# A Hymba decoder layer on one core: the output projection with w_out split once and its tiles one by one

## The chip, the cores and the metric

The kernel runs on one core of a Trainium2 chip. The metric is the device time of one execution in microseconds, the median of several runs. The engines are named as the profile names them: PE (matmuls; PEld is its weight load), DVE and POOL (element-wise on vectors), ACT (scalar functions and copies) and SP, which here issues the DMAs.

## The reference

One decoder layer, x of 1024 rows (S) by 1024 columns (D), all in float32:

```python
proj = x @ w_in                                   # 3072 columns: q, k, v, gate B, gate C, h
attn = rmsnorm(softmax(q1 k1^T) v - lam * softmax(q2 k2^T) v)   # 4 heads, causal
conv = B * causal_dwconv3(C * h)
mix  = concat([attn, conv], -1) @ w_out           # 512 + 512 columns, w_out is 1024 x 1024
h1   = layer_norm(ALPHA * x + mix, ln1_g, ln1_b)
up   = h1 @ w_up                                  # 2 x 2816 columns: gate, value
f    = (silu(causal_dwconv3(gate) + cb) * value) @ w_down
out  = layer_norm(ALPHA * h1 + f, ln2_g, ln2_b)
```

## The kernel before, in words

**Products.** Every float32 operand is split into a "hi" part, rounded to the type that PE takes (a cast on ACT, L63), and a "lo" part, the rest (a subtraction on DVE, or on POOL where `eng` says so, L64). A product is three matmuls, hi by hi, hi by lo and lo by hi (`mm3`, L72 to L74). The large products go by 2x2 blocks in seven products instead of eight (`pair`, L103 ff.). For the FFN the seven operands of h1 are "11", "21", "22" and the differences "t1", "t2", "t3", "t4", each a hi and a lo tile of `[128, 4, 512]` in `hb`. In them h1 stands transposed (its columns on the partitions).

**Order.** The code is written in one order and a scheduler places each engine's instructions; each engine then runs its own list in order. Tiles live in pools, and an instruction that writes a tile waits until the tile that held the memory before has been read.

**The output projection** (from L517 on) takes cat, the concatenation, from eight DRAM blocks `cat_d[k]` of 128 columns each, stored by the attention (`cat_d[0..3]`, L371) and by the convolution (`cat_d[4..7]`, `gate_out`, L471 and L472). `cat_d[3]` and `cat_d[7]` are the last to be stored. The k-blocks are taken in `K_ORDER = (4, 5, 0, 1, 2, 6, 7, 3)`. Row tiles of 128 rows stand in three groups, of tiles 0 to 2, 3 to 5 and 6 to 7. Each group goes over all eight k: `weights` (L591) loads w_out's block k (L593) and splits it in two halves, the group's part of cat is loaded (L612) and split into `ch` and `cl`, and each tile gets six matmuls into its two PSUM banks. `REUSE = 2` blocks are kept from one group to the next, so 20 of the 24 times a block is loaded and split again; in the third group five of them split their lo on POOL (`POOL_LO`). The second group goes over k in the reverse order. After a group, each tile's sum (L635: ALPHA x + the product), its layer norm (L539 to L547) and its turning follow, put off into the next group at three places (`NORM_AT`).

**The turning.** `first_half` (tiles 0 to 3) transposes a tile's eight 128x128 blocks on PE (L552) and splits them into "11" and "21". `second_half` and `combine` (tiles 4 to 7) transpose too and make the differences from the transposed blocks: old values are put together again on POOL (L573), t1, t2 and t3 are DVE subtractions out of PSUM, t4 is on POOL. For tiles 5 to 7 that waits until after the early gates.

**The early gates.** The FFN's first four pairs (`NEARLY = 4`) need only "11" and "21" for their gate half; those 96 matmuls run before the operands of the second half are done. Pair 0's sums `s1_0` and its difference are prepared there (`wu0` is its w_up block). Then pairs 0 to 21 run whole, and the down projection follows.

**The start.** x's eight tiles `xt`, in the right-hand pool `ini`, feed the operands `xb` of the input projection. Then the pairs of the input projection run interleaved with the attention, with their temporaries (s1, p1, ...) in the pool `wab`.

Of the kernel before, what the change touches and what calls it, by code (L numbers as in the profile page):

```python
# [46 lines left out]
def layer_kernel(ctx: ExitStack, tc: tile.TileContext, x, xt, w_in, w_v, lam, vecs, w_out, ln, w_up, w_down, out):  # L47
# [507 lines left out]
    def first_half(src, t):  # L555
        ts = slice(t * P, (t + 1) * P)
        for k0, n in ((0, "11"), (4, "21")):
            split(hb[n][0][:, :, ts], hb[n][1][:, :, ts], transposed(src, k0))

    def second_half(src, t):  # L560

        b_ = [transposed(src, k0) for k0 in (0, 4)]
        return lambda: combine(t, *b_)

    def combine(t, b12, b22):
        ts = slice((t - 4) * P, (t - 3) * P)

        def put(n, v, eng=None):
            split(hb[n][0][:, :, ts], hb[n][1][:, :, ts], v, eng=eng)

        def old(n, tag, bufs=1):
            v = cp.tile([P, 4, P], F32, name=f"o{n}", tag=tag, bufs=bufs)
            G.tensor_tensor(v, hb[n][0][:, :, ts].bitcast(F32), hb[n][1][:, :, ts].bitcast(F32), op=ALU.add)  # L573
            return v

        t1 = old("11", "tb0", 2)
        t4 = old("21", "tb2")
        V.tensor_tensor(t1, b12, t1, op=ALU.subtract)
        put("t1", t1)
        t2 = cp.tile([P, 4, P], F32, name="t2", tag="tb1")  # L580
        V.tensor_tensor(t2, b22, t1, op=ALU.subtract)
        put("t2", t2)
        put("22", b22)
        t3 = cp.tile([P, 4, P], F32, name="t3", tag="tb0", bufs=2)
        A.copy(t3, b12)
        V.tensor_tensor(t3, b22, t3, op=ALU.subtract)
        put("t3", t3)
        G.tensor_tensor(t4, t4, t2, op=ALU.subtract)
        put("t4", t4, G)

    def weights(t0, k, eng):  # L591
        raw = e0.tile([P, D], F32, name=f"wo{t0}_{k}_r", tag="wg", bufs=NWG)
        SQ.dma_start(raw, w_out[k * P:(k + 1) * P, :])  # L593
        wo = [e0.tile([P, 2, 512], F32R, name=f"wo{t0}_{k}_{d}", tag="ring", bufs=RING[0]) for d in range(2)]
        for d in range(2):
            split(wo[d][:, 0, :], wo[d][:, 1, :], raw[:, d * 512:(d + 1) * 512], eng=eng)
        return wo

    pending, late, held = [], [], {}
    for t0 in (0, 3, 6):  # L600
        tt = list(range(t0, min(t0 + 3, NT)))
        w = len(tt) * P
        acc = {(t, d): bank(f"op{t}_{d}") for t in tt for d in range(2)}
        order = K_ORDER if t0 != 3 else K_ORDER[::-1]
        for ki, k in enumerate(order):
            if ki < REUSE and t0:
                wo = held[k]
            else:
                wo = weights(t0, k, G if ki in POOL_LO and t0 == 6 else None)
            held[k] = wo  # L610
            cr = cc.tile([P, 384], F32, name="cr", tag="cr", bufs=4)
            SQ.dma_start(cr[:, :w], cat_d[k][:, t0 * P:t0 * P + w])  # L612
            ch = cc.tile([P, 384], F32R, name="ch", tag="ch", bufs=2)
            cl = cc.tile([P, 384], F32R, name="cl", tag="cl", bufs=2)
            split(ch[:, :w], cl[:, :w], cr[:, :w])
            if ki == 0:
                xr = {}
                for t in tt:
                    xr[t] = cx.tile([P, D], F32, name=f"xr{t}", tag="xr", bufs=4)
                    SQ.dma_start(xr[t], x[t * P:(t + 1) * P, :])  # L620
            if ki == 1 and t0 == 0:
                g1 = bcast_row(cp, 0, "g1")
                b1 = bcast_row(cp, 1, "b1")
            for i, t in enumerate(tt):
                s_ = slice(i * P, (i + 1) * P)
                for d in range(2):
                    mm3(acc[t, d], ch[:, s_], cl[:, s_], wo[d][:, 0, :], wo[d][:, 1, :], ki == 0, ki == 7)
            if pending and ki in NORM_AT:
                pending.pop(0)()
        while pending:  # L630
            pending.pop(0)()
# [327 lines left out]
```

## Time and profile before

| | us |
|---|---|
| median of 3 runs (1128.56 to 1128.86) | 1128.77 |
| the profiled execution | 1129.07 |
| span of its core in the trace | 1127.3 |
| PE busy | 1084.9 |
| DVE busy | 906.4 |
| ACT busy | 522.5 |
| POOL busy | 147.6 |

The span is what the trace covers; the profiled execution's own time is 1.8 us longer. Matmuls overlap in PE's pipeline: one that is listed with 0.39 us starts 0.23 us after the one before it, and a busy PE is not PE at its peak. In a row of the waits, the engine and the line that waited stand ahead of the arrow and the one waited for behind it. The granted clock of 1.00 is 2.4 GHz, 0.50 is 1.2 GHz.

### The profile page before, as it was taken

To read this page: it belongs to the slowest core of one execution; us is meant where nothing else is said; L and a number is where in the kernel's file an instruction comes from. 1 tells how busy PE (TensorE), PEld (TensorE's weight loads), DVE (VectorE), ACT (ScalarE), POOL (GpSimd) and SP (SyncE) were. 2 spreads that over 40 slices of the span, in tenths; PEclk is the share of its full clock that TensorE was granted. 3 is DMA by queue.
4 is the path that set the end of the run, shared out by engine and by line. 5 is a ranking of instruction groups with operands and counts; after the bars stand their busy time and mean duration, and the time that the engine had idled before them with its cause. 6 is when DMAs were issued, how large, how long until landed. Compare 5 with 4: busy or idle time off the path is not lost.

```text
span 1127.3 us, 13854 instructions
## 1 busy us (share of the span) xinstructions
PE 1084.9 (96%) x4940; PEld 873.8 (78%) x4940; DVE 906.4 (80%) x1393; ACT 522.5 (46%) x980; POOL 147.6 (13%) x182
## 2 busy tenths in 40 slices
PE   7999999999999999879999999999999999999996
PEld 6777877876768888668888888888888887788885
DVE  7678898689787688998967676777777599997797
ACT  6357586386675333445433334333333333444540
POOL 0002213013031224760000000000000000000102
PEclk9999999999999999999999999999999999999998
DMA  7421201301206754423232212131312295111111
GB/s 267 150 94 43 85 25 52 115 21 52 75 29 197 279 177 159 154 75 113 94 112 70 99 59 109 57 113 57 112 56 93 78 383 220 38 66 38 46 67 75
DMA packets 50421, 118.53 MB, mean 105 GB/s; under 512 B 5040, under 2 KB 18480, under 8 KB 50352
## 3 DMA queue, kind: packets, MB, share of 16 engines
q1 hardware_dynamic: 50352, 117.64, 29.7%
q8 instruction: 39, 0.64, 0.2%
q14 instruction: 30, 0.25, 0.1%
HBM read 90.88 MB, written 26.74 MB: 104 GB/s over the span
## 4 chain that ended last, share of the span: by engine, by line
PE 71%; DVE 15%; ACT 5%; POOL 3%; DMA 3%; issue 2%; SPq 0%; POOLq 0%; DVEq 0%; ACTq 0%
PE X L74 8%; PE X L72 8%; PE X L73 8%; PE Z L74 5%; PE Z L73 5%; PE Z L72 5%; PE dx L73 2%; PE dx L74 2%; PE dx L72 2%; PE op L74 2%; PE op L73 2%; PE op L72 2%; DVE a L64 2%; PE dz L74 2%; PE dz L72 2%
## 5 line engine op out<-in xcount | busy, mean ns | idle before, releaser
L64 DVE TENSOR_TENSOR a<-s,a 128x512 fp32r<-128x512 f32 x118 | 85.3, 724 | 45.3 <-ACT a L63 44.3
L63 ACT CAST a<-s 128x512 fp32r<-128x512 f32 x118 | 73.3, 623 | 94.5 <-PE X L74 43.0
L63 ACT CAST a<-w 128x512 fp32r<-128x512 f32 x106 | 65.9, 623 | 87.3 <-PE X L74 40.4
L64 DVE TENSOR_TENSOR a<-w,a 128x512 fp32r<-128x512 f32 x102 | 72.3, 710 | 22.6 <-ACT a L63 22.2
L63 ACT CAST T<-b 128x512 fp32r<-128x512 f32 x66 | 40.6, 621 | 68.4 <-PE dz L74 33.9
L73 PE MATMUL dx<-T,S 128*128 128x512 f32 x176 | 69.0, 392 | 1.2 <-DVE T L64 1.2
L74 PE MATMUL dx<-T,S 128*128 128x512 f32 x176 | 68.5, 389 | 0.0
L72 PE MATMUL dx<-T,S 128*128 128x512 f32 x176 | 66.0, 391 | 0.0
L64 DVE TENSOR_TENSOR T<-b,T 128x512 fp32r<-128x512 f32 x66 | 45.0, 685 | 16.3 <-ACT T L63 16.3
L74 PE MATMUL op<-wo,cl 128*128 128x512 f32 x128 | 51.2, 400 | 3.2 <-DVE cl L64 3.2
L444 DVE TENSOR_REDUCE nm<-sc 128x1 f32<-128x128 f32 (+5 forms) x64 | 47.5, 750 | 7.7 <-PE sc L443 7.3
L709 POOL MEMSET gs<- 128x2 f32 x22 | 2.2, 99 | 379.6 <-DVE t L728 379.6
L73 PE MATMUL dz<-T,S 128*128 128x512 f32 x132 | 51.8, 393 | 0.0
L74 PE MATMUL dz<-T,S 128*128 128x512 f32 x132 | 51.5, 390 | 0.0
L72 PE MATMUL op<-wo,ch 128*128 128x512 f32 x128 | 51.3, 401 | 0.0
L448 ACT ACTIVATE p<-sc,nm 128x128 f32<-128x128 f32 (+5 forms) x64 | 47.6, 745 | 7.2 <-DVE p L457 4.1
L73 PE MATMUL op<-wo,ch 128*128 128x512 f32 x128 | 50.8, 397 | 0.0
L72 PE MATMUL dz<-T,S 128*128 128x512 f32 x132 | 48.4, 393 | 0.5 <-ACT T L63 0.5
L729 ACT ACTIVATE t<-t 128x1024 f32<-128x1024 f32 x22 | 23.4, 1062 | 51.9 <-DVE t L728 51.9
L441 PE MATMUL sc<-k,q 128*128 128x512 f32 (+2 forms) x96 | 37.1, 394 | 7.1 <-ACT p L448 6.1
L366 POOL TENSOR_TENSOR me<-me,y 128x256 f32<-128x256 f32 x16 | 12.5, 783 | 236.0 <-ACT y L365 236.0
L63 ACT CAST wo<-wo_r 128x512 fp32r<-128x512 f32 x40 | 24.4, 619 | 40.9 <-PE op L74 37.8
(314 smaller groups left out, 3374.9 us busy)
## 6 DMA issues: line engine op xcount, KB each, us to landing
w<-in_w_up SPq DMA_DIRECT2D x44, 512.0 KB, 3.2
b<-in_w_down SPq DMA_DIRECT2D x44, 256.0 KB, 6.9
w<-in_w_in SPq DMA_DIRECT2D x20, 512.0 KB, 3.4
wo_r<-in_w_out SPq DMA_DIRECT2D x20, 512.0 KB, 4.8
act_d<-act SPq DMA_DIRECT2D x19, 512.0 KB, 2.6
ra<-act_d SPq DMA_DIRECT2D x19, 512.0 KB, 7.0
v_d<-vs SPq DMA_DIRECT2D x16, 256.0 KB, 2.7
vhl<-v_d SPq DMA_DIRECT2D x8, 512.0 KB, 4.6
```

Source lines behind the costliest of these rows:

```text
L63: A.copy(hi, src)
L64: (eng or V).tensor_tensor(lo, src, hi.bitcast(F32), op=ALU.subtract)
L72: T.matmul(ps, lh, rh, start=first, stop=False, **kw)
L73: T.matmul(ps, lh, rl, start=False, stop=False, **kw)
L74: T.matmul(ps, ll, rh, start=False, stop=last, **kw)
L366: G.tensor_tensor(me, me, y, op=ALU.mult)
L441: T.matmul(sc[:, bs], q2[m][:, qs], k2[m][:, bs], start=True, stop=False)
L444: V.tensor_reduce(nm[:, m:m + 1], sc[:, :n], axis=AX.X, op=ALU.max, negate=True)
L448: A.activation(pt[:, :n], sc[:, :n], AF.Exp, bias=nm[:, m:m + 1], accum_out=sm[:, m:m + 1])
L709: G.memset(gs[:, 0:2], 0.0)
L729: A.activation(t_, t_, AF.Silu)
```

## The change

It rewrites the output projection, its turning and the order of the early gates, and gives three pools new bounds.

**w_out** is split once. Each k-block becomes one tile `[128, 4, 512]` (hi in the first two quarters, lo in the others) by one 1024-wide cast and one 1024-wide subtraction. These tiles lie in pools `hop0` to `hop3`, in the places that the operands t2, 22, t3 and t4 take later. All lo subtractions are DVE's. The raw blocks go through `wtile`: three slots of `wraw`, which now lives through the whole kernel, and two of a new pool.

**cat** is split in halves of 512 columns (`mixer`): eight blocks for tiles 0 to 3, eight for tiles 4 to 7, and a half is kept until its tiles are done.

**The tiles.** 0 and 1 go over k together, with `weights` and `mixer` beside them; then 2 to 7 go one by one over the kept blocks. The dictionary `then` says after which k of which tile something else is issued.

**The turning.** For tiles 4 to 7 the differences are made by rows before the transposes, from the tile's own rows and from tile t - 4's, which come back from h1's copy in DRAM (`old_rows`, and `b21` in `late`): `diff` holds t1 and then t2. Each operand then has its own group of four transposes. The early gates are cut in halves (`gate_half`), between which these groups stand.

**The start.** x's tiles lie in two pools, five and three, and the temporaries of the input projection's pairs in a pool `wtmp` of their own.

```diff
-    hb = {n: [hop.tile([P, 4, 512], F32R, ...) for c in "hl"] for n in OPS}
+    late_p = [pool(f"hop{n}", hop_st) for n in range(4)]
+    LATE_OPS = ("t2", "22", "t3", "t4")
...
+    xpl = [pool(f"xs{i}", st0, side="right") for i in range(2)]
+    xs = {t: xpl[i // 5].tile([P, NK, P], F32, name=f"xt{t}", tag="xt", bufs=(5, 3)[i // 5])
+          for i, t in enumerate(VORDER)}
...
-        return pair(wp, wp, wa, wb, xb, X, Z, None, c11, c12, lean=True)
+        return pair(wp, wt_, wa, wb, xb, X, Z, None, c11, c12, lean=True)
...
+    def put(n, t, v):
+        if n not in hb:
+            pl = late_p[LATE_OPS.index(n)] if n in LATE_OPS else hop
+            hb[n] = [pl.tile([P, 4, 512], F32R, ...) for c in "hl"]
+        ts = slice(t % 4 * P, (t % 4 + 1) * P)
+        split(hb[n][0][:, :, ts], hb[n][1][:, :, ts], v)
+    def weights(i):
+        k = K_ORDER[i]
+        raw = wtile([P, 2, 512], f"wo{k}_r")
+        SQ.dma_start(raw, w_out[k * P:(k + 1) * P, :].rearrange("p (a b) -> p a b", a=2))
+        w = late_p[i // 2].tile([P, 4, 512], F32R, ...)
+        split(w[:, 0:2], w[:, 2:4], raw)
+        wo[k] = w
+    def mixer(i, half):
+        k = K_ORDER[i]
+        cr = cc.tile([P, 512], F32, name="cr", tag="cr", bufs=3)
+        SQ.dma_start(cr, cat_d[k][:, half * 512:(half + 1) * 512])
+        ...
+        split(c[:, 0], c[:, 1], cr)
+        cat[half, k] = c
+    def norm_diff(t):
+        norm(t)
+        V.tensor_tensor(diff[t], xr[t][:, 0:512], diff[t], op=ALU.subtract)
+    def second_half(t):
+        v = diff[t]
+        put("t1", t, transposed(v, 0))
+        V.tensor_tensor(v, xr[t][:, 512:D], v, op=ALU.subtract)
+    def late(n, t):
+        r = xr[t]
+        if n == "t2":
+            src = diff[t]
+        elif n == "22":
+            src = r[:, 512:D]
+        elif n == "t3":
+            src = r[:, 0:512]
+            V.tensor_tensor(src, r[:, 512:D], src, op=ALU.subtract)
+        else:
+            src = cc.tile([P, 512], F32, name=f"b21_{t}", tag="cr", bufs=3)
+            SQ.dma_start(src, h1_d[t - 4][:, 512:D])
+            V.tensor_tensor(src, src, diff[t], op=ALU.subtract)
+        put(n, t, transposed(src, 0))
+    then = {(2, 2): [lambda: norm(1)], (2, 5): [lambda: first_half(0)], (3, 2): [lambda: first_half(1)],
+            (3, 6): [lambda: first_half(2)], (4, 5): [lambda: first_half(3)], (7, 4): [lambda: gate_parts(0)],
+            (7, 7): [lambda: gate_parts(1)]}
+    for i in range(NK):
+        then.setdefault((3, i), []).append(lambda i=i: mixer(i, 1))
+    for t in range(4, NT - 1):
+        then.setdefault((t + 1, 6), []).insert(0, lambda t=t: second_half(t))
+    for t in range(2):
+        rows(t)
+    for i in range(NK):
+        weights(i)
+        mixer(i, 0)
+        ...
+        for t in range(2):
+            mms(t, i)
+    for t in range(2, NT):
+        rows(t)
+        ...
+        for i in range(NK):
+            mms(t, i)
+            for f in then.get((t, i), ()):
+                f()
+    norm_diff(NT - 1)
+    gate_half(0, False)
+    gate_half(0, True)
+    gate_parts(2)
+    for t in (4, 5, 6):
+        late("t2", t)
+    gate_half(1, False)
+    second_half(7)
+    for t in (4, 5, 6):
+        late("22", t)
+    late("t2", 7)
+    late("22", 7)
...
```

**How it moves instructions.** SP's queue at the last stores of cat, before: `cat_d_66` and `cat_d_70` are the blocks k = 3 and k = 7, `wo_3_r` a raw block of w_out, `g` and `b` the norm's rows, `cr` a part of cat.

```order
L612 DMA cr<-cat_d_69 128x384
L593 DMA wo_7_r<-in_w_out 128x1024
L371 DMA cat_d_66<-osb 128x256
L593 DMA wo_3_r<-in_w_out 128x1024
L472 DMA cat_d_70<-w_3616 128x512 x2
L533 DMA g_3754<-in_ln 128x1024
L533 DMA b_3756<-in_ln 128x1024
L593 DMA wo_6_r<-in_w_out 128x1024
L612 DMA cr<-cat_d_70 128x384
L593 DMA wo_2_r<-in_w_out 128x1024
L612 DMA cr<-cat_d_66 128x384
```

The same place now (`w_4504` is a gate block of w_up, `xr` are rows of x):

```order
L372 DMA cat_d_66<-osb 128x256
L660 DMA w_4504<-in_w_up 128x1024
L604 DMA xr_3708<-in_x 128x1024
L604 DMA xr_3712<-in_x 128x1024
L473 DMA cat_d_70<-w_3627 128x512 x2
L547 DMA g_3748<-in_ln 128x1024
L547 DMA b_3750<-in_ln 128x1024
L592 DMA cr<-cat_d_70 128x512
L592 DMA cr<-cat_d_66 128x512
L604 DMA xr_3896<-in_x 128x1024
```

Between the two stores stand three loads instead of one, and the reloads of k = 7 and k = 3 follow behind `g` and `b`.

DVE's list at the convolution's last product (L471 before, L472 now, the two halves of `cat_d[7]`), before:

```order
L465 SCALAR_TENSOR_TENSOR w_3616<-u_3358,cols,w_3616 128x1024
L466 SCALAR_TENSOR_TENSOR w_3616<-u_3358,cols,w_3616 128x1024
L471 TENSOR_TENSOR w_3616<-X_3493,w_3616 128x512
L471 TENSOR_TENSOR w_3616<-p_3529,w_3616 128x512
L64 TENSOR_TENSOR wo_1_1_3811<-wo_1_r,wo_1_1_3811 128x512
L64 TENSOR_TENSOR cl<-cr,ch 128x384
L64 TENSOR_TENSOR wo_2_0_3842<-wo_2_r,wo_2_0_3842 128x512
```

The same place now; `c_7` and `c_3` are the splits of cat's blocks, `s_0` is pair 0's `s1_0`, `xr_3708` are tile 0's rows:

```order
L61 TENSOR_TENSOR wo_3832<-wo_r,wo_3832 128x1024
L466 SCALAR_TENSOR_TENSOR w_3627<-u_3369,cols,w_3627 128x1024
L61 TENSOR_TENSOR c_6_3837<-cr,c_6_3837 128x512
L467 SCALAR_TENSOR_TENSOR w_3627<-u_3369,cols,w_3627 128x1024
L61 TENSOR_TENSOR wo_3854<-wo_r,wo_3854 128x1024
L472 TENSOR_TENSOR w_3627<-X_3504,w_3627 128x512
L472 TENSOR_TENSOR w_3627<-p_3540,w_3627 128x512
L61 TENSOR_TENSOR wo_3876<-wo_r,wo_3876 128x1024
L61 TENSOR_TENSOR c_7_3859<-cr,c_7_3859 128x512
L61 TENSOR_TENSOR c_3_3881<-cr,c_3_3881 128x512
L737 TENSOR_TENSOR s_0_4669<-w_4667 128x512
L617 SCALAR_TENSOR_TENSOR xr_3708<-xr_3708,op_0_3710 128x512
```

Two subtractions for w_out (1024 wide) and one for cat stand among the convolution's operations, where before these followed each other, and `s_0` stands ahead of tile 0's sum.

PE's list among the early gates, before (the eight transposes of tile 6):

```order
L72 MATMUL Y_4670<-hb_21h,a 128x512
L73 MATMUL Y_4670<-hb_21l,a 128x512
L74 MATMUL Y_4670<-hb_21h,a 128x512
L552 MATMUL trp<-ident,xr_4320 128x128 x8
L72 MATMUL X_4717<-hb_11h,a 128x512
L73 MATMUL X_4717<-hb_11l,a 128x512
```

And now, behind the first half of gate 1 (`diff_4370` is tile 7's difference, the `xr` are rows of tiles 4 to 6 and, the last, of tile 7):

```order
L71 MATMUL X_4535<-hb_11h,a 128x512
L566 MATMUL trp<-ident,diff_4370 128x128 x4
L566 MATMUL trp<-ident,xr_4128 128x128 x4
L566 MATMUL trp<-ident,xr_4210 128x128 x4
L566 MATMUL trp<-ident,xr_4289 128x128 x4
L566 MATMUL trp<-ident,diff_4370 128x128 x4
L566 MATMUL trp<-ident,xr_4366 128x128 x4
L69 MATMUL Y_4603<-hb_21h,a 128x512
```

Six groups of four transposes stand in a row, where before eight transposes stood together.

## Rows read from the trace of the kernel before

**Rows 1.** The page: busy time of two engine streams; w_up's loads, issue to landing

```profile
PE 1084.9 (96%) x4940; PEld 873.8 (78%) x4940; DVE 906.4 (80%) x1393; ACT 522.5 (46%) x980; POOL 147.6 (13%) x182
...
w<-in_w_up SPq DMA_DIRECT2D x44, 512.0 KB, 3.2
```

**Rows 2.** Busy time by stretch: busy us and count per engine, PE's clock, DMA share, GB/s

```profile
370.00:440.00 70.00, 70.00 (x315) 56.64 (x314) 51.77 (x75) 24.59 (x49) 18.19 (x16) 1.00 0.62 217
440.00:540.00 100.00, 88.36 (x377) 69.57 (x376) 93.53 (x122) 45.64 (x82) 47.67 (x38) 0.95 0.33 115
540.00:580.00 40.00, 40.00 (x177) 32.78 (x176) 32.22 (x46) 15.39 (x25) 0.20 (x2) 1.00 0.22 79
```

**Rows 3.** Timeline of PE: start, length (us), line, operation; eight transposes and the next matmul

```profile
415.83 1.04 PE L552 MATMUL trp<-ident,xr 128*128 128x128 f32 x8
416.63 0.48 PE L72 MATMUL op<-wo,ch 128*128 128x512 f32 x1
```

**Rows 4.** Busy time by stretch: first and last of three at half the clock

```profile
461.98:465.39 3.41, 2.96 (x11) 2.24 (x11) 3.41 (x5) 2.23 (x6) 3.33 (x3) 0.50 0.60 244
...
506.36:509.77 3.41, 3.41 (x9) 2.65 (x9) 2.65 (x5) 1.24 (x3) 0.74 (x2) 0.50 0.00 0
```

**Rows 5.** Waits of PE, 368 to 580 us: total, times, longest; the two longest

```profile
PE op L74 <- DVE cl L64: 3.2, 3, 2.2
PE X L72 <- ACT t L585: 2.3, 1, 2.3
```

**Rows 6.** Groups by line, 440 to 476 us: busy us, mean ns of one, idle before

```profile
L64 POOL TENSOR_TENSOR wo<-wo_r,wo 128x512 fp32r<-128x512 f32 x7 | 12.0, 1731 | 9.2 <-ACT wo L63 9.2
...
L546 DVE SCALAR_TENSOR_TENSOR xr<-xr,mv,g 128x1024 f32<-128x1024 f32 x3 | 4.6, 1540 | 0.0
...
L64 DVE TENSOR_TENSOR wo<-wo_r,wo 128x512 fp32r<-128x512 f32 x2 | 3.5, 1761 | 0.0
```

**Rows 7.** Timeline of DVE: the convolution's last product, then tiles 0 to 2's norm chain

```profile
374.13 0.71 DVE L471 TENSOR_TENSOR w<-p,w 128x512 f32<-128x512 f32 x1
374.76 0.68 DVE L64 TENSOR_TENSOR wo<-wo_r,wo 128x512 fp32r<-128x512 f32 x1
...
400.02 3.40 DVE L635 SCALAR_TENSOR_TENSOR xr<-xr,op 128x512 f32<-128x512 f32 x5
...
406.19 0.19 DVE L541 BATCH_NORM_AGGREGATE mv<-st 128x2 f32<-128x12 f32 x1
...
408.51 1.28 DVE L547 SCALAR_TENSOR_TENSOR xr<-xr,rs,b 128x1024 f32<-128x1024 f32 x1
```

**Rows 8.** Timeline of PE: the output projection's first matmul

```profile
369.63 0.39 PE L72 MATMUL op<-wo,ch 128*128 128x512 f32 x1
```

**Rows 9.** Timeline of SP's queue: the last two stores of cat

```profile
377.87 0.32 SPq L371 DMA_DIRECT2D cat_d<-osb  x1
...
378.76 0.88 SPq L472 DMA_DIRECT2D cat_d<-w  x2
```

**Rows 10.** Landings: the store at 377.9; those at 378.8; reloads 384 to 386; DMA 379 to 392

```profile
DMA to landing us min/median/max: 2.0/2.0/2.0
...
DMA to landing us min/median/max: 4.9/5.1/5.2
...
DMA to landing us min/median/max: 5.3/6.1/6.9
...
DMA packets 1726, 4.70 MB, mean 362 GB/s; under 512 B 190, under 2 KB 599, under 8 KB 1726
```

**Rows 11.** Timeline of ACT: a cast of 512 columns

```profile
385.93 0.62 ACT L63 CAST wo<-wo_r 128x512 fp32r<-128x512 f32 x1 [2.64 <-PE op L74]
```

**Rows 12.** The start of head 0: PE's two waits, and the stretch behind them

```profile
56.87 0.50 PE L72 MATMUL X<-xb_11h,a 128*128 128x512 f32 x1 [1.24 <-ACT a L63]
...
58.27 0.51 PE L74 MATMUL X<-xb_11h,a 128*128 128x512 f32 x1 [0.68 <-DVE a L64]
...
59.22:62.62 3.40, 3.40 (x10) 2.61 (x9) 2.28 (x4) 0.95 (x2) 0.00 (x0) 0.50 0.65 199
```

More of the change, by code (lines that the diff above doesn't have):

```diff
@@ L37 @@
 NTHIRD = 7
-POOL_LO = (2, 3, 4, 5, 6)
-REUSE = 2
 RMS_AT = [(c, 1) for c in range(4)]
-NORM_AT = (2, 3, 5)
 K_ORDER = (4, 5, 0, 1, 2, 6, 7, 3)
@@ L320, in layer_kernel @@
     at = pool("at", ab, side="right")
+    wt_ = pool("wtmp", ab, side="right")
     wp = pool("wab", ab, side="right")
@@ L520, in layer_kernel @@
     e0 = pool("e0", p8_st)
+    ew = pool("ew", p8_st, side="right")
+    late_p = [pool(f"hop{n}", hop_st) for n in range(4)]
     hop = pool("hop", hop_st)
@@ L553, in transposed @@
         return ps
[L555 to L594, printed above, removed]
-        for d in range(2):
[L596 to L631, printed above, removed]
-        for t in tt:
-            for d in range(2):
-                ds_ = slice(d * 512, (d + 1) * 512)
-                V.scalar_tensor_tensor(xr[t][:, ds_], xr[t][:, ds_], ALPHA, acc[t, d], op0=ALU.mult, op1=ALU.add)
-        def norm(t, r):
-            layer_norm(cp, r, r, g1, b1)
-            SQ.dma_start(h1_d[t], r)
-        def turn(t, r):
-            if t < 4:
-                first_half(r, t)
-            elif t == 4:
-                second_half(r, t)()
-            else:
-                late.append(second_half(r, t))
-        rows_ = [(t, xr[t]) for t in tt]
-        pending = [(lambda a=a: (norm(*a), turn(*a))) for a in rows_]
@@ new lines, in layer_kernel, with rows @@
+    cat = {}
+    def mixer(i, half):
+        k = K_ORDER[i]
+        cr = cc.tile([P, 512], F32, name="cr", tag="cr", bufs=3)
+        SQ.dma_start(cr, cat_d[k][:, half * 512:(half + 1) * 512])
+        if i < NK - 1:
+            c = e0.tile([P, 2, 512], F32R, name=f"c{half}_{k}", tag="ring", bufs=RING[0])
+        else:
+            c = cx.tile([P, 2, 512], F32R, name=f"c{half}_{k}", tag="c8")
+        split(c[:, 0], c[:, 1], cr)
+        cat[half, k] = c
+    xr, acc = {}, {}
+    def rows(t):
+        xr[t] = cx.tile([P, D], F32, name=f"xr{t}", tag="xr", bufs=5)
+        SQ.dma_start(xr[t], x[t * P:(t + 1) * P, :])
+        acc[t] = [bank(f"op{t}_{d}") for d in range(2)]
@@ new lines, in mms, with norm @@
+    def mms(t, i):
+        k = K_ORDER[i]
+        c, w, ts = cat[t // 4, k], wo[k], slice(t % 4 * P, (t % 4 + 1) * P)
+        for d in range(2):
+            mm3(acc[t][d], c[:, 0, ts], c[:, 1, ts], w[:, d], w[:, 2 + d], i == 0, i == NK - 1)
+    def norm(t):
+        r = xr[t]
+        for d in range(2):
+            ds_ = slice(d * 512, (d + 1) * 512)
+            V.scalar_tensor_tensor(r[:, ds_], r[:, ds_], ALPHA, acc[t][d], op0=ALU.mult, op1=ALU.add)
+        layer_norm(cp, r, r, g1, b1)
+        SQ.dma_start(h1_d[t], r)
@@ new lines, in gate_half @@
+    def gate_half(f, second):
+        if not second:
+            X = bank(f"X{f}")
+            block_product(e0, X, None, hb, "11", True, gates[f][1])
+            p1 = gp.tile([P, 512], F32, name=f"p1_{f}", tag="p1", bufs=1)
+            A.copy(p1, X)
+            early[f] = [X, p1]
+        else:
+            X, p1 = early[f]
+            Y = bank(f"Y{f}")
+            block_product(e0, Y, None, hb, "21", True, gates[f][2])
+            c11 = gp.tile([P, 512], F32, name=f"c11_{f}", tag="c11", bufs=NEARLY)
+            V.tensor_tensor(c11, Y, p1, op=ALU.add)
+            early[f] = gates[f][0], X, c11
@@ L846, in layer_kernel @@
     Z = [bank(f"dz{t}") for t in range(4)]
-    rw = [e0.tile([P, 2, 512], F32, name=f"rw{t}", tag="wg", bufs=NWG) for t in range(4)]
+    rw = [wtile([P, 2, 512], f"rw{t}") for t in range(4)]
     r11 = residual(0, c0, [r[:, 0, :] for r in rw])
```

85 lines of the change are left out of this document (58 added, 27 removed).

## The prediction

> **What bounds the kernel now.** I read four views in this order: the page, the busy time by stretch, TensorE's (PE's) waits, and the order of single instructions where a wait sits. The page shows one core whose PE is busy for 96% of the span [rows 1], so a change pays only through what it does to PE's stream: fewer instructions, fewer gaps, or fewer stretches at the lower clock.
>
> The stretches say where such a gain is [rows 2]. In 370 to 440 us, the first half of the output projection, PE never idles: 315 instructions, 24 of them transposes, in 70 us. A transpose costs 0.80/8 = 0.10 us (eight start at 415.83, the next matmul at 416.63, [rows 3]), so a 128x512 matmul costs (70 - 2.4)/291 = 0.232 us. In 540 to 580 us, plain FFN, 177 matmuls take 40 us: 0.226 us each. The stretch between holds 377 instructions: by the code 40 transposes, 75 projection matmuls and 262 of the FFN. At those prices it needs 4.0 + 17.4 + 59.2 = 80.6 us, and it lasts 100. So **19.4 us are lost between 440 and 540 us**. About 14 of them are gaps (PE is busy for 88.4, and a busy PE includes overlapping ends). The rest comes with three stretches of 3.41 us at half the clock, of which the first and the last are in [rows 4]; each costs half its length, 1.7 us.
>
> Who makes PE wait there: DVE, mostly (PE's six waits from 368 to 580 us are 11.4 us together; the two longest are in [rows 5]). DVE is busy for 93.5 of the 100 us [rows 2], and with only 122 instructions. Its "lo" subtraction of a 128x512 block takes 1.76 us beside a busy POOL, which takes 1.73 for the same job [rows 6]; the same subtraction took DVE 0.68 at 374.76, where POOL had only small blocks to do [rows 7]. POOL is busy for 47.7 of these 100 us. So the loss is one of DVE and POOL together: the third row group splits w_out again on both, and every row tile of the second half makes its differences after the transposes, partly on POOL.
>
> **What the change removes.** Eight w_out blocks are split instead of twenty, POOL splits nothing, and POOL's `old` and `t4` sums are gone. In the new order DVE has 105 operations of 512 columns, 16 of 1024 and 8 small ones between the sums of tile 0 and the last early gate. At 0.63 us (from one 512-wide operation's start to the next one's), 1.28 (a 1024-wide one) and 0.19, all in [rows 7], that is 66.2 + 20.5 + 1.5 = 88 us. PE needs for the same part six tiles of 48 matmuls (66.8), 112 transposes (11.2) and 96 gate products (21.7), about 100 us. DVE is then no longer the bound, and I take the whole loss as gone: **-19.4**. What can remain of it is priced below, as handshakes and in two rivals.
>
> **What it adds on PE.** The matmuls are as many as before. The sums are made in rows and then transposed, so t1, t2, 22, t3 and t4 each need their own transposes: 112 instead of 64, 48 x 0.10 = **+4.8**. They cannot hide, PE being the bound.
>
> **A new wait at the seventh k.** Before, three tiles shared each k-block: 18 matmuls, 4.2 us. Now two do: 12 x 0.232 = 2.8 us. PE begins the projection at 369.63 [rows 8] and comes to the seventh block (k = 7) at 369.6 + 6 x 2.8 = 386.4, instead of 394.8. That block is the last one that the convolution writes. SP waits for POOL's norm chain until 377.87, then stores `cat_d[3]`; before, the `cat_d[7]` store followed at 378.76 [rows 9]. Two things make it later. Its product on DVE (374.13 in [rows 7]) now has three 1024-wide and two 512-wide lo subtractions mixed in ahead of it, 3 x 1.28 + 2 x 0.63 = 5.1 us, so it ends near 379.9. And SP issues three loads of 512 KB between the two stores (a gate block and x's rows 0 and 1), where before there was one. The store then goes out at about 380.1. Landing: it took 4.9 to 5.2 us behind one load, against 2.0 for a store alone [rows 10]. Two more loads at that stretch's 362 GB/s are 2.9 us, less the 1.2 us by which they start earlier: 6.8, so 386.9. The reload of 256 KB comes back 3.1 us later (the page's median load takes 3.2, [rows 1]), at 390.0, and the cast that PE needs takes 0.62 [rows 11]: 390.6 against 386.4, **+4.2**. The lower end is 0: a store at 2.0 and a reload at 2.4 would land at 384.5, in time. The upper end is 7.5: the store at 6.8, the reload at 6.1 like the reloads of before in this stretch [rows 10]. I take the middle because the store has less ahead of it than those reloads had.
>
> **A second wait, for tile 0's transposes.** DVE's order has `s1_0`, a sum for FFN pair 0, ahead of tile 0's sums, and `s1_0` needs the load of w22. SP issues that only after the reloads of the second half of cat, of which the third waits for a slot until c0_3 is split (about 392); so it is issued near 393.5. With 5.1 us to land, as for the store behind a load [rows 10], it is there at 398.6. After `s1_0` (0.6), tile 0's chain with tile 1's sums mixed in is seven narrow operations, a small one, two wide ones and some 0.4 for POOL's root, 4.4 + 0.2 + 2.6 + 0.4 = 7.6 us: 406.8. PE wants those rows after two more k-blocks of tiles 0 and 1 and six of tile 2: 390.6 + 5.6 + 8.4 = 404.6. **+2.2**, between 0 (w22 lands in 3.2) and 5 (the chain at the 9.8 us that it took from 400.02 to 409.79 with three tiles mixed, [rows 7]).
>
> **Handshakes at the end.** Tile 7's chain is split by the first gate's `c11`, which waits for PE; `diff7` is then about 1.5 us late for its second transposes, and the others (diff6, b21_7) come out even. **+1.5**, from 0 to 7.5 (the third rival). SP's stores of h1 and its reloads lie beside this work.
>
> **The start.** x's early tiles get a pool of their own and the pairs' temporaries too, so the first operand of head 0's first product is split earlier. Before, PE waits 1.24 and 0.68 us there, and runs at half the clock for 3.40 us right after [rows 12]. Gone: 1.9 and 1.7. But in the new order ACT copies X's result before it casts `s1` for the next product, so that one waits for both behind the last matmul, some 0.5 + 0.62 + 0.2 = 1.3 us. 1.3 - 1.9 - 1.7 = **-2.3**, from 0 (the wait only moves) to -3.6.
>
> **Everything else** is nothing, within 0.5: the attention of heads 1 to 3 and the FFN from pair 4 have the same order. The down projection starts behind the last pair in both kernels, so a shift moves it whole.
>
> **The sum:** -19.4 + 4.8 + 4.2 + 2.2 + 1.5 - 2.3 = -9.0. From the profiled 1129.07 us that is 1120.1, and the median of the runs lies 0.3 lower: **1119.8**, with an own range of 1116 to 1123.5.
>
> **The rivals.**
> - *The loads land in time.* Both new waits are zero: 1119.8 - 6.4 = 1113.4. For it: a store alone took 2.0 us. Against: it isn't alone here. Chance 0.18.
> - *Banks and evacuations hold PE at the end.* After the last tile 16 groups of transposes each need a free bank, a cast (0.62) and a subtraction (0.68) with three or four banks free; if each costs its own 0.36 us again, 16 x 0.36 = 6: 1125.8. For it: before, PE waited for just such an evacuation chain (2.3 for `t` at L585, [rows 5]). Against: 88 us of DVE in 100. Chance 0.17.
> - *Transposes in a row lower the clock.* Before, at most eight stand together (0.8 us), and the matmuls after them come at the full pace [rows 3]; now 24 do in one place (2.4 us), and 8 to 12 in others. If three such places each brought the 3.41 us at half the clock that a gap brings now [rows 4], that is 3 x 1.7 = 5.1: 1124.9. Chance 0.07. The Trainium skill states such a rule (TensorE: Matmul & The Clock Gate, section Part 4: PE-mode transpose): a transpose doesn't count as PE-busy in the way a matmul does. The trace neither shows nor excludes it for a row of 24.
> - *Slower: DVE stays slow.* If DVE's pace between 440 and 540 is its own and not POOL's doing, the new part runs at 93.5/122 = 0.77 us for a narrow operation [rows 2] and 1.54 for a wide one [rows 6]: 105 x 0.77 + 16 x 1.54 + 1.5 = 107, 7 over PE's 100, and the 5.7 us of handoffs (half of the 11.4) stay too: +12.7, 1132.5. With the handoffs it turns the sign where the part takes 103.3 us, a narrow mean of (103.3 - 26.1)/105 = 0.74. For it: 128x1024 operations were slow there too. Against: all those slow rows stand beside a busy POOL, which now has only the norms' roots. Chance 0.09.
> - *The start does not change* (the pools aren't what held the first split): 1122.1, inside the forecast's own range, no case of its own.
>
> **How the numbers follow.** Forecast 0.46, then 0.18, 0.17, 0.07 and 0.09, and 0.03 for what I don't see. The range goes from below the second case (1112) to above the third (1127), and leaves out the slow DVE and the edges. 0.2% (2.3 us) is about what a measurement of this kernel can tell from no change. Faster than 1126.5: the first two cases whole, four fifths of the third and most of the fourth, with a discount for what isn't seen, 0.80; within 0.2%: 0.08; slower: 0.12.
>
> **What would show it.** Right: about 110 us from PE's first projection matmul to pair 0's first Z product, POOL near idle there, DVE's lo subtractions at 0.7 us or for two halves 1.3; one wait of about 4 us for k = 7's cast near 386, one of 2 us before tile 0's transposes near 404; no stretch at half the clock at 59 us. Wrong: DVE busy for over 95% between 440 and 490 us, half-clock stretches right behind the runs of transposes, or a wait for k = 7 beyond 8 us, which would pull x's later rows and w22 along.

## The result: slower by 0.6%, where faster by 0.8% was forecast

The changed kernel takes 1134.76 us (median of 4 runs, 1134.05 to 1135.86) against 1128.66 for the kernel before: a ratio of 1.0056, 95% interval 1.0038 to 1.0073. That is slower beyond the 0.2% that can be told apart, and outside the forecast's range of 1112 to 1127. The profiled execution took 1134.05 us.

The page of the changed kernel, its span and first row:

```profile
span 1132.3 us, 13779 instructions
...
PE 1087.0 (96%) x4988; PEld 879.3 (78%) x4988; DVE 889.4 (79%) x1375; ACT 505.0 (45%) x936; POOL 105.6 (9%) x152
```

The span is 5.0 us longer than before. To see where, I took each interval between two starts on PE, less the usual one for that shape (0.227 us for 512 columns, 0.109 for a transpose, 0.12 for 256 columns), and added up by stretch. This is the time that PE loses to waits and to the lower clock:

| us lost by PE | before | changed | best version below |
|---|---|---|---|
| 0 to 100 | 12.2 | 10.6 | 10.9 |
| 100 to 150 | 5.1 | 9.1 | 5.3 |
| 150 to 369.5 | 21.4 | 22.4 | 21.5 |
| 369.5 to 540 | 21.5 | 18.1 | 1.3 |
| from 540 on | 4.1 | 4.1 | 4.0 |
| sum | 64.3 | 64.4 | 43.0 |

The losses are as large as before, and 48 more transposes make up the 5.0 us (48 x 0.10 = 4.8). So the expected gain did come, and as much was lost again elsewhere. The busy time by stretch shows both (columns as in [rows 2]):

```profile
370.00:400.00 30.00, 23.19 (x97) 18.68 (x96) 15.67 (x17) 6.22 (x9) 7.88 (x5) 0.89 0.71 247
400.00:440.00 40.00, 37.02 (x174) 30.16 (x172) 26.94 (x41) 7.89 (x14) 4.68 (x6) 1.00 0.57 194
440.00:540.00 100.00, 96.51 (x461) 80.23 (x462) 82.51 (x122) 33.51 (x59) 9.84 (x13) 0.98 0.22 80
```

Between 440 and 540 us PE now issues 461 instructions instead of 377 [rows 2], with POOL at 9.8 us instead of 47.7. But from 370 to 400, where before there was no gap, PE works 23.2 of 30 us. Its waits from 350 to 600 us, the whole list but for one of 0.2:

```profile
PE op L69 <- ACT c L60: 6.8, 1, 6.8
PE trp L566 <- DVE xr L561: 6.5, 2, 4.0
```

**The wait for k = 7** is 6.8 us long. SP's queue there (start, length, line, operation):

```profile
383.30 0.33 SPq L372 DMA_DIRECT2D cat_d<-osb  x1
383.71 0.38 SPq L660 DMA_DIRECT2D w<-in_w_up  x1
384.15 0.92 SPq L604 DMA_DIRECT2D xr<-in_x  x2
385.17 0.87 SPq L473 DMA_DIRECT2D cat_d<-w  x2
...
392.05 0.80 SPq L592 DMA_DIRECT2D cr<-cat_d  x2
...
393.84 4.49 SPq L592 DMA_DIRECT2D cr<-cat_d  x3
...
398.86 0.90 SPq L660 DMA_DIRECT2D w<-in_w_up  x2
```

The store of `cat_d[3]` goes out at 383.30, and the loads of w2, xr0 and xr1 and the store of `cat_d[7]` wait behind it, though that product is done on DVE at 382.7. The store lands 6.8 us later, the reload goes out at 392.05, and PE goes on at 396.68, with 3.41 us at half the clock (the granted clock, 0.50, is the third number from the end of the second row):

```profile
396.68 0.79 PE L69 MATMUL op<-wo,c 128*128 128x512 f32 x1 [6.81 <-ACT c L60]
...
396.68:400.09 3.41, 3.41 (x8) 2.69 (x9) 1.30 (x2) 0.58 (x1) 0.00 (x0) 0.50 0.99 375
```

**The two waits for normalised rows** are tile 0's (2.4 us at 414.67) and one that the prediction doesn't have, tile 3's (4.04 us at 443.49, with half the clock for 3.4 us after it). DVE's timeline ahead of each:

```profile
407.29 0.69 DVE L737 TENSOR_TENSOR s<-w 128x512 f32<-128x512 f32 x1 [9.30 <-DMA w<-in_w_up]
...
431.71 0.69 DVE L61 TENSOR_TENSOR c<-cr,c 128x512 fp32r<-128x512 f32 x1 [3.02 <-ACT c L60]
...
434.87 0.69 DVE L61 TENSOR_TENSOR c<-cr,c 128x512 fp32r<-128x512 f32 x1 [1.86 <-ACT c L60]
...
436.08 1.28 DVE L61 TENSOR_TENSOR c<-cr,c 128x512 fp32r<-128x512 f32 x2
437.28 1.28 DVE L617 SCALAR_TENSOR_TENSOR xr<-xr,op 128x512 f32<-128x512 f32 x2
```

DVE stands still for 9.3 us in front of `s1_0`, which waits for w22, with tile 0's sums behind it. Later it stands still for 3.0 and 1.9 us in front of splits of cat's second half, with tile 3's sums behind those. The reloads that those splits wait for had themselves waited on SP's queue for slots that earlier splits free (410 to 440 us):

```profile
SPq L592 <- DVE c L61: 3.8, 4, 1.4
```

**In head 0** (ACT's timeline) a copy of `osb` waits for the store of the `osb` before it to land, and the cast that PE needs stands behind the copy:

```profile
104.24 0.37 ACT L420 COPY osb<-o 128x256 f32<-128x256 f32 x1 [3.53 <-DMA cat_d<-osb]
...
105.82 0.41 ACT L60 CAST sqh<-sq 128x256 fp32r<-128x256 f32 x1
```

PE waits 3.67 us for that cast. Behind it, too, 3.4 us are at half the clock.

### The profile page after: what moved, and what is told of

It is laid out like the page before. It is cut to its first block, busy times and chain, and to the rows that moved or that the text cites. A ratio compares the mean times of both kernels' runs of the same rounds, so it can differ in the third digit from the quotient of the medians.

```text
span 1132.3 us, 13779 instructions
## 1 busy us (share of the span) xinstructions
PE 1087.0 (96%) x4988; PEld 879.3 (78%) x4988; DVE 889.4 (79%) x1375; ACT 505.0 (45%) x936; POOL 105.6 (9%) x152
## 4 chain that ended last, share of the span: by engine, by line
PE 53%; DVE 6%; DMA 3%; issue 1%; POOL 0%; SPq 0%; POOLq 0%; DVEq 0%; ACT 0%; ACTq 0%
PE X L69 7%; PE X L70 7%; PE X L71 7%; PE Z L70 4%; PE Z L69 4%; PE Z L71 4%; PE dx L70 2%; PE dx L71 2%; PE dx L69 2%; PE Y L69 2%; PE dz L70 2%; PE Y L70 2%; PE Y L71 2%; PE dz L71 2%; PE dz L69 2%; DMA b<-in_w_down 1%
## 5 line engine op out<-in xcount | busy, mean ns | idle before, releaser
L61 DVE TENSOR_TENSOR a<-w,a 128x512 fp32r<-128x512 f32 x106 | 74.1, 702 | 16.1 <-ACT a L60 15.8
L69 PE MATMUL op<-wo,c 128*128 128x512 f32 x128 | 52.0, 407 | 6.8 <-ACT c L60 6.8
L70 PE MATMUL op<-wo,c 128*128 128x512 f32 x128 | 51.3, 400 | 0.0
L71 PE MATMUL op<-wo,c 128*128 128x512 f32 x128 | 51.0, 398 | 0.0
L70 PEld LDWEIGHTS dx<-T,S 128*128 128x128 f32 x176 | 33.0, 188 | 9.6 <-DVE T L61 2.9
L69 PEld LDWEIGHTS dx<-T,S 128*128 128x128 f32 x176 | 33.0, 188 | 7.4 <-ACT T L60 0.6
```

The lines of the kernel that those rows point to most:

```text
L61: (eng or V).tensor_tensor(lo, src, hi.bitcast(F32), op=ALU.subtract)
L69: T.matmul(ps, lh, rh, start=first, stop=False, **kw)
L70: T.matmul(ps, lh, rl, start=False, stop=False, **kw)
L71: T.matmul(ps, ll, rh, start=False, stop=last, **kw)
```

## The experiments

The theory: four waits (k = 7, tile 0, tile 3, head 0) with their half-clock stretches ate the gain, each for a reason of its own, and without them the projection is faster by what was forecast for it. The ratios are to the kernel before:

| version | ratio | 95% interval | us against before |
|---|---|---|---|
| changed kernel | 1.0056 | 1.0038 to 1.0073 | +6.3 |
| start_old | 1.0009 | 0.9998 to 1.0019 | +1.0 |
| late_turns | 0.9987 | 0.9976 to 0.9998 | -1.5 |
| three_tiles | 0.9954 | 0.9937 to 0.9970 | -5.2 |
| cr_four | 1.0023 | 1.0009 to 1.0036 | +2.6 |
| store_act | 1.0013 | 1.0001 to 1.0026 | +1.5 |
| store_pool | 1.0007 | 0.9995 to 1.0019 | +0.8 |
| before_start | 1.0036 | 1.0024 to 1.0047 | +4.1 |
| best_three | 0.9888 | 0.9862 to 0.9914 | -12.6 |
| best_two | 0.9900 | 0.9885 to 0.9916 | -11.3 |
| three_start | 0.9910 | 0.9896 to 0.9924 | -10.1 |
| three_all | 0.9873 | 0.9857 to 0.9889 | -14.3 |

### start_old and before_start: the start alone

```diff
-    xs = {t: xpl[i // 5].tile([P, NK, P], F32, ..., bufs=(5, 3)[i // 5])
+    xs = {t: ini.tile([P, NK, P], F32, ..., bufs=NT)
...
-        return pair(wp, wt_, wa, wb, xb, X, Z, None, c11, c12, lean=True)
+        return pair(wp, wp, wa, wb, xb, X, Z, None, c11, c12, lean=True)
```

> The changed kernel with x's eight early tiles in one pool again and the temporaries of the input projection's pairs back in the pool wab; every engine's list up to the end of the attention is then that of the kernel before. Theory (the start costs what it shows): the new start gains 1.6 us before 100 us but brings a 3.8 us wait of PE at 102 us, for an ACT cast queued behind the copy of osb, and 1.7 us of half clock after it. Undone: 1134.8 - 4.0 - 1.1 + 1.6 = 1131.3 us, and no wait of PE over 2 us between 95 and 115 us. Rival (the wait at 102 us comes from the landing of a store and not from the new order): it stays, and the time is 1134.8 + 1.6 = 1136.4 us.

The other way round, the kernel before with only these two edits of the change:

> The kernel before with only the new start: two pools for x's early tiles and an own pool for the pairs' temporaries. All lists up to the end of the attention are then those of the changed kernel. Theory (the start alone is a loss): 1.6 us less before 100 us, then PE's wait of 3.7 us near 102 and half clock, 4 to 5 us more between 100 and 150 and 1 more later: 3.4 to 4.4 us slower than the kernel before. Rival (the wait near 102 is there only with the kept pool wraw or something else of the changed projection): 1.6 us faster.

Undone, the time is 5.3 us lower (3.5 were expected), with the wait at 102 us gone. Alone in the kernel before, the new start costs 4.1 us. There (before_start) ACT's timeline has the same row again:

```profile
102.34 0.37 ACT L422 COPY osb<-o 128x256 f32<-128x256 f32 x1 [3.54 <-DMA cat_d<-osb]
```

and of PE's waits from 55 to 115 us the longer of two is:

```profile
PE mq L361 <- ACT sqh L63: 3.7, 1, 3.7
```

So the start's pools are a loss by themselves, in either kernel. In the kernel before, each of the two edits alone (x's pools, the pool `wtmp`) leaves every engine's list as it was; only both together move it.

### late_turns: PE asks later for tiles 0, 1 and 3

```diff
-    then = {(2, 2): [lambda: norm(1)], (2, 5): [lambda: first_half(0)], (3, 2): [lambda: first_half(1)],
-            (3, 6): [lambda: first_half(2)], (4, 5): [lambda: first_half(3)], ...
+    then = {(2, 2): [lambda: norm(1)], (3, 0): [lambda: first_half(0)], (3, 3): [lambda: first_half(1)],
+            (3, 6): [lambda: first_half(2)], (5, 3): [lambda: first_half(3)], ...
```

> The changed kernel with the transposes of tiles 0, 1 and 3 placed later in PE's list (after k-block 0 and 3 of tile 3, and after k-block 3 of tile 5), nothing else moved in the code. Theory (the two waits for a normalised row are PE asking too early): the 2.6 us wait near 412 and the 4.2 us wait near 439 with its 1.8 us of half clock go: 1134.8 - 8.6 = 1126.2 us. The wait of about 7 us for k = 7 near 390 stays. Rival (DVE is so late there that the wait only moves, to the next thing PE needs from it): less than 3 us gained, 1132 to 1135, with a new wait of PE between 412 and 450 us.

The gain is 7.8 us of the 8.6, and from 400 to 440 us PE has no gap, and later there is one wait of 0.4 us:

```profile
400.00:440.00 40.00, 40.00 (x187) 33.10 (x186) 26.76 (x40) 7.89 (x14) 4.68 (x6) 0.99 0.58 202
```

DVE was late only for the place at which PE asked. The wait for k = 7 stays, at 6.4 us.

### store_act and store_pool: what holds the store

```diff
-        SQ.dma_start(cat_d[h][:, c * QC:(c + 1) * QC], osb)
+        (A if h == H - 1 and c == 3 else SQ).dma_start(cat_d[h][:, c * QC:(c + 1) * QC], osb)
```

> The changed kernel with one DMA moved and nothing else: the last store of cat_d[3], which waits for POOL's norm chain, is issued from ACT, which is idle there for 19 us, instead of from SP. Theory (that store holds SP's queue, and behind it stand the loads of w2, xr0 and xr1 and the store of cat_d[7]): SP issues the three loads near 374 instead of 384, and the store of cat_d[7] when its product is ready, near 382.7 instead of 385.2, with nothing ahead of it; it lands in 2 to 3 us instead of 6.8, the reload is back before 389, PE's wait of 7 us for k = 7 and the half clock behind it go: -8.6, and w22 comes some 6 us earlier, so the wait near 412 goes too (-2.6): 1123.5 us by the scale of 1134.8 for the changed kernel, 5 us under the kernel before. Rival (the DMA engines' rate there makes the store and the reload slow): the wait stays above 3 us, a gain under 4 us.

SP's queue, the landing of `cat_d[7]`'s two stores, one of SP's waits, and PE's waits from 360 to 600 us:

```profile
373.76 3.33 SPq L660 DMA_DIRECT2D w<-in_w_up  x2
377.14 0.90 SPq L604 DMA_DIRECT2D xr<-in_x  x2
382.74 0.93 SPq L473 DMA_DIRECT2D cat_d<-w  x2
...
388.93 0.80 SPq L592 DMA_DIRECT2D cr<-cat_d  x2
```

```profile
DMA to landing us min/median/max: 2.1/2.4/2.7
```

```profile
SPq L592 <- DMA cat_d<-osb: 4.1, 1, 4.1
```

```profile
PE trp L566 <- DVE xr L561: 4.3, 2, 2.2
PE op L69 <- ACT c L60: 1.8, 1, 1.8
```

With that one DMA moved, the three loads go out 7 us earlier (376.8 to 377.6, the first of them the second in the first row; near 374 was expected), the store as soon as its product is ready, and it lands in 2.1 to 2.7 us, as expected. The wait for k = 7 falls from 6.8 to 1.8 us, so the head of SP's queue made most of it. But the reload goes out at 388.93 and not at 386: it waits 4.1 us for the *other* store, that of `cat_d[3]`. Tile 0's wait stays, 2.2 us, since PE is early by what it gained; tile 3's falls from 4.0 to 2.1. Behind the waits of 1.8 and 2.2 us stand 3.4 us each at half the clock, where in the changed kernel the 2.4 us for tile 0 had none behind them. The gain is 4.8 us, not 11.

For the reload's wait I formed a new theory and moved the store once more, to POOL (`G` for `A` in the diff):

> The changed kernel with the last store of cat_d[3] issued from POOL instead of SP (in store_act it was ACT); nothing else differs. In store_act PE still waited 1.8 us for k = 7: both halves of cat_d[7] had landed near 386.0, but SP's reload went out at 388.9, just when the store of cat_d[3] landed. Theory (the reload of k = 7 waits for the store of cat_d[3], because the program's list gives DMAs issued from SP and ACT eight completion semaphores in turn and a DMA waits for the one eight places before it; a DMA issued from POOL is not in that turn): SP's reload goes out at 385.5 to 386.5, and PE's wait for k = 7 is under 0.3 us, with no half clock behind it. Rival (the reload went out late because the stores of cat_d[7] themselves were late behind the transfers): SP's reload stays at 388 or later and the wait at 1.5 us or more. The time: 0 to 3 us less than store_act, since PE then asks up to 2 us earlier for tile 0's rows.

SP's queue, the two reloads' landing, and PE's waits from 360 to 600 us in store_pool:

```profile
382.13 0.93 SPq L473 DMA_DIRECT2D cat_d<-w  x2
383.15 0.41 SPq L547 DMA_DIRECT2D g<-in_ln  x1
383.62 0.45 SPq L547 DMA_DIRECT2D b<-in_ln  x1
384.28 0.92 SPq L592 DMA_DIRECT2D cr<-cat_d  x2
```

```profile
DMA to landing us min/median/max: 6.3/6.5/6.6
```

```profile
PE trp L566 <- DVE xr L561: 5.8, 2, 3.7
PE op L69 <- ACT c L60: 1.3, 1, 1.3
```

The shared completion semaphore is confirmed as what held the reload: it goes out 4.6 us earlier, and even before my estimate. The trace of store_act shows the sharing itself: the landings of all DMAs of SP and ACT are told by eight semaphores in turn, and the store from ACT and the reload have the same one. Still the wait is 1.3 us and not 0, because the reload now goes out right behind 1 MB of `g` and `b` and takes 6.5 us instead of the 2.9 that it took in store_act, where it went out 4.7 us behind them. So the semaphore's part and the transfers' part of that wait lie one behind the other, and both expectations for it were half wrong. Tile 0's wait grows to 3.7 us, and the time is that of store_act within the intervals.

### cr_four: more slots for the reloads

```diff
-        cr = cc.tile([P, 512], F32, name="cr", tag="cr", bufs=3)
+        cr = cc.tile([P, 512], F32, name="cr", tag="cr", bufs=4)
...
-            src = cc.tile([P, 512], F32, name=f"b21_{t}", tag="cr", bufs=3)
+            src = cc.tile([P, 512], F32, name=f"b21_{t}", tag="cr", bufs=4)
```

> The changed kernel with four slots instead of three for the reloaded blocks of cat. Theory (SP stands still with a reload that waits for a slot, and the load of w22 that DVE's s1_0 needs stands behind it): SP issues w22 some 3.5 us earlier, it lands near 404 instead of 407, PE's wait of 2.6 us near 412 goes, and the one near 439 shrinks by 0 to 4: 1129 to 1132 us. Rival (those transfers are held by the DMA engines' rate, 4 MB in 12 us there, not by the slot): w22 lands at 406.5 to 407.5 again and the time stays within 1 us of 1134.8.

The time lies in the theory's range, but only in part for its reason. SP stands still there all the same, with one reload more ahead of w22:

```profile
392.45 5.50 SPq L592 DMA_DIRECT2D cr<-cat_d  x4
...
398.47 0.90 SPq L660 DMA_DIRECT2D w<-in_w_up  x2
```

w22 goes out 0.4 us earlier, not 3.5, and DVE's `s1_0` starts at 405.80 instead of 407.29. The waits for tiles 0 and 3 are 3.2 us together instead of 6.5. Another part of the gain is in the wait for k = 7 (5.0 us instead of 6.8), with only one load between the two stores in the new list. This run doesn't tell the two theories of the slots apart.

### three_tiles: PE comes to k = 7 later

```diff
-    for t in range(2):
+    for t in range(3):
         rows(t)
...
-        for t in range(2):
+        for t in range(3):
             mms(t, i)
-    for t in range(2, NT):
+    for t in range(3, NT):
         rows(t)
...
-    then = {(2, 2): [lambda: norm(1)], (2, 5): [lambda: first_half(0)], ...
+    then = {(3, 2): [lambda: norm(1)], (3, 5): [lambda: norm(2)], (4, 0): [lambda: first_half(0)],
+            (4, 3): [lambda: first_half(1)], (4, 6): [lambda: first_half(2)], (5, 3): [lambda: first_half(3)], ...
```

> The changed kernel with tiles 0, 1 and 2 over k together (18 matmuls for each k-block instead of 12), then 3 to 7 one by one; norms and transposes of tiles 0 to 3 come correspondingly later. Theory (PE comes to k = 7 too early by 7 us, and each wait adds its length): PE comes there 8.4 us later, so the wait of 7 us near 390 and the 1.8 us of half clock behind it go, as do those near 412 and 439: 1134.8 - 8.8 - 8.6 = 1117.4 us. Rival (the loads and DVE's chain behind the late store are the true bound, so the waits move back): a wait of 4 us or more appears between 406 and 425 us, and the time is above 1122.

The gain is 11.5 us of the 17.4. The wait for k = 7 and those for tiles 0 and 3 are gone, and there is none of more than 0.7 us between 370 and 440. So the rival's wait isn't there, though the time, 1122.8 us, is above its 1122. What PE lost from 369.5 to 540 us falls from 18.1 to 5.0 us; left or new are 1.6 us for tile 4's difference at 446 and single steps of 0.7 and less. The other 2 us are in the attention, which this version doesn't touch: its execution lost 1.2 us more between 100 and 150 and 1.4 more between 300 and 350. That is the clock. Behind the same wait of 3.7 us near 106, PE worked for 6.3 us at half the clock, where it was 3.4 in the changed kernel; and 3.4 us at half the clock stand behind a wait of 2.0 us near 336, which the changed kernel has too (2.0 us), with the clock at 1.00 behind it. In three_tiles:

```profile
105.25:112.08 6.83, 6.32 (x19) 5.04 (x20) 4.55 (x7) 3.01 (x8) 0.00 (x0) 0.50 0.01 2
...
337.36:340.77 3.41, 3.41 (x11) 2.63 (x11) 2.49 (x5) 2.30 (x5) 1.74 (x3) 0.50 0.01 2
```

### The versions put together

best_three is three_tiles with start_old and cr_four; three_start is the same without cr_four; three_all is best_three with store_act. best_two keeps two tiles over k and has start_old, late_turns, store_act and cr_four.

> The changed kernel with the old start, tiles 0 to 2 over k together, later transposes of tiles 0 to 3, and four slots for cat's reloads. By sums of the single runs against the kernel before: three tiles -5.2, old start -3.5 to -5.3, four slots -0.5: 9 to 11 us faster than the kernel before. If the loads behind the late store are the bound after all, the earlier projection finds the same wait again and the old start gains under 1.5 here: 6 to 7 us faster.

> The changed kernel with tiles 0 and 1 together as they are, the old start, the last store of cat_d[3] from ACT, later transposes of tiles 0, 1 and 3, and four slots for cat's reloads. If the store in SP's queue is the cause of the wait for k = 7, this is as fast as the version with three tiles: 9 to 12 us faster than the kernel before, and PE has no wait over 1 us between 370 and 480 us. If the wait for k = 7 stays, 3 to 5 us slower than that version.

> The version with the old start, tiles 0 to 2 over k together and later transposes, but cat's reloads in three slots as in the changed kernel. Theory (with PE coming to k = 7 later, SP's standstill at the reload slots holds back nothing that PE waits for, but for a difference of tile 4 near 444): 0 to 2 us slower than with four slots, 10.5 to 12.6 us faster than the kernel before. Rival (the slots are what made the version with three tiles so much faster than the sum of its parts): 4 us or more slower than with four slots.

> The version with the old start, tiles 0 to 2 over k together, later transposes, four slots, and the last store of cat_d[3] issued from ACT. Theory (once PE comes to k = 7 after the reload, an earlier store gives nothing): within 1 us of the same version with that store on SP, 12 to 13 us faster than the kernel before. Rival (the waits that are left in the projection hang on that queue): 1 to 2 us faster still.

best_three is 12.6 us faster than the kernel before, best_two 11.3: two ways around the wait for k = 7 come to the same, within their intervals. best_three gained a little more than the sum of the singles, 9 to 11 us; its interval, 9.7 to 15.6, holds most of that range. In best_two the longest wait of PE from 360 to 600 us is 0.8 us. three_start is 2.5 us behind best_three, somewhat more than expected, but their intervals overlap; in its trace a wait of 1.5 us for tile 4's difference is back. three_all has no wait of PE at all from 360 to 600 us, and its stretches are full:

```profile
370.00:440.00 70.00, 70.00 (x328) 58.04 (x327) 49.80 (x69) 12.35 (x21) 14.34 (x15) 1.00 0.64 219
440.00:540.00 100.00, 99.91 (x478) 82.83 (x477) 86.51 (x128) 41.62 (x71) 6.20 (x10) 1.00 0.24 85
```

It is 14.3 us faster than the kernel before (12.5 to 16.1), the best of all. Whether it beats best_three (-12.6) isn't settled; the intervals overlap. In the traces, the 1.3 us that PE still waited there in best_three are gone.

## Why the prediction was wrong, step by step

- **The 19.4 us lost in 440 to 540: right.** They were 19.7 by the table's measure, and are 2.3 in the changed kernel, 1.7 of it the half clock behind tile 3's wait (the wait itself began at 439 and is counted ahead of 440). three_all puts the forecast's two structural terms to the test: -19.4 + 4.8 = -14.6, measured -14.3. In its profiled execution the span is 16.7 us shorter: by the table, 20.2 less lost from 369.5 to 540, 5.0 more for transposes, and 1.3 less before 100 us, where its lists are those of the kernel before. DVE is at its fast pace: in the changed kernel `L560` took 1.28 us from 440 to 476, where `L546` took 1.54 [rows 6]. The rival "DVE stays slow" is out. (The prediction's "six waits" there are six groups, of eight waits; the 11.4 us hold.)

```profile
L560 DVE SCALAR_TENSOR_TENSOR xr<-xr,mv,g 128x1024 f32<-128x1024 f32 x4 | 5.1, 1283 | 0.1
```

- **The 48 transposes, +4.8: right**; with equal losses the spans differ by 5.0.
- **The wait for k = 7, +4.2: mechanism right, 2.6 too small, and its half clock was left out.** The wrong step is "SP waits for POOL's norm chain until 377.87", taken over from the trace of before. PE begins the projection 3.8 us later (373.39 instead of 369.63), which shifts all. But the store of `cat_d[3]` comes 5.4 us later, at 383.30: POOL's five operations take 8.2 us (375.04 to 383.27), where they took 6.6 before, in both cases from 1.65 us after PE's start on. No run shows why they got slower. DVE's product wasn't the limit: two wide subtractions stood among its operations, not three, and it was done 9.3 us after PE's start, 10.3 in the forecast. The store of `cat_d[7]` goes out 11.8 us after that start instead of the 10.5 forecast. Its landing was the 6.8 of the forecast; the reload took 4.1 instead of 3.1. That gives 4.2 + 1.3 + 1.0 = 6.5 of the 6.8. And the 3.41 us at half the clock cost 1.7 more: I had seen that shorter gaps bring them in the kernel before [rows 4, 12], and priced them only in a rival. The first of POOL's five operations, in the kernel before and now:

```profile
371.29 1.04 POOL L366 TENSOR_TENSOR me<-me,y 128x256 f32<-128x256 f32 x1 [20.20 <-ACT y L365]
```

```profile
375.04 1.65 POOL L367 TENSOR_TENSOR me<-me,y 128x256 f32<-128x256 f32 x1 [20.20 <-DVE w L465]
```

- **Tile 0's wait, +2.2: right** (2.4), and for the reason given: `s1_0` waits for w22 till 407.29. That the number fits is luck. Counted from PE's start, w22 was there 4.9 us later than forecast (it took 7.9 us to land, not 5.1), PE asked 3.9 us later, behind the longer wait for k = 7 and its half clock, and DVE's part took 0.9 less.
- **Tile 3's wait: missing**, 4.0 us and 1.7 of half clock. I followed DVE's list up to tile 0's sums and took the rest as a sum of work, 88 us in 100. A sum of work doesn't show an order: eight splits of reloaded blocks stand ahead of tile 3's sums, and DVE stood still for two of them. late_turns shows that this cost time only because of the place at which PE asked.
- **The handshakes at the end, +1.5:** nothing; PE had no wait from 480 to 540 us.
- **The start, -2.3: right where I looked** (the wait for `a` is 1.2 us and no half clock is left near 60 us), **and "everything else is nothing" was the wrong step behind it.** The lists differ from 39 to 134 us, and I set that at nothing without reading it. There lay 4 to 5 us, more than the start's gain. The 1.7 us for the half clock were no fixed price either. start_old, three_all and best_three have the old start with the same two waits of 1.24 and 0.68 us. The clock fell behind them in the first two and not in best_three (three_all, then best_three):

```profile
57.20:60.61 3.41, 3.41 (x10) 2.66 (x9) 2.66 (x5) 0.62 (x1) 0.00 (x0) 0.50 0.70 189
```

```profile
58.50:62.00 3.50, 3.28 (x14) 2.69 (x15) 2.75 (x5) 0.84 (x2) 0.00 (x0) 1.00 0.77 198
```

- **The rival on transposes in a row** is out: 24 stand together from 492.37 to 494.94, and the matmuls after them follow each other at 0.23 us with the granted clock at 1.00. The Trainium skill (TensorE: Matmul & The Clock Gate, section Part 4: PE-mode transpose) says that a transpose doesn't count as PE-busy in the way a matmul does. In a row of this length between matmuls the trace shows no price of that.

```profile
492.37 0.60 PE L566 MATMUL trp<-ident,diff 128*128 128x128 f32 x4
492.81 1.47 PE L566 MATMUL trp<-ident,xr 128*128 128x128 f32 x12
...
494.58 0.60 PE L566 MATMUL trp<-ident,xr 128*128 128x128 f32 x4
...
495.25 0.40 PE L70 MATMUL Y<-hb_21l,a 128*128 128x512 f32 x1
495.49 0.39 PE L71 MATMUL Y<-hb_21h,a 128*128 128x512 f32 x1
...
480.00:500.00 20.00, 20.00 (x114) 17.11 (x113) 19.26 (x32) 9.36 (x18) 2.04 (x3) 1.00 0.09 34
```

By size: k = 7 cost 4.3 us more than forecast with its half clock (6.8 + 1.7 - 4.2), tile 3 cost 5.7 (4.0 + 1.7), head 0 4.0 and the attention behind it 1.0, against 1.5 less at the end: 13.5 of the 14 us between the forecast's -9.0 and the measured +5.0 of the span.

## What to carry to other kernels

When a stage is made shorter, everything that was hidden by its length is asked for earlier: look for the next store, reload and row that it asks for, and what stands ahead of each in its queue. A sum of work on an engine says only that it isn't the bound; what PE waits for is set by what stands in front of one instruction in that engine's list. A queue whose head waits for a slow chain should not carry the transfers that others wait for: one store moved to an idle engine's queue took 5 of 7 us off a wait. Half clock behind a short wait is a chance, not a fixed sum: price it as one, and look at it in more than one execution before a difference of 2 us is put down to an edit. Of a DMA's waits read also the completion semaphore that it shares with an earlier one.
